# One tile ahead: out-projections before the norm, and the feed-forward part's first product before the last casts

## The chip, the cores and the metric

The program runs on one core of one Trainium2 chip. The metric is the device time of one execution in microseconds, the median of several runs. The profile and all rows come from one execution of the kernel before.

## The reference

One layer of a hybrid streaming encoder over 2048 prompt tokens and 64 sample tokens (hidden size 1024), all in float32. Token mixing is sliding-window attention beside a chunked spatial gate; what follows it matters here:

```python
def _merge(attn_o, cmlp_o, norm_attn_g, norm_cmlp_g, w_out):
    cat = jnp.concatenate([_rmsnorm(attn_o, norm_attn_g), _rmsnorm(cmlp_o, norm_cmlp_g)], -1)
    return cat @ w_out

def _post(x, mix, ln1_g, ln1_b, w_gate_up, w_down, ln2_g, ln2_b):
    h = _layernorm(ALPHA * x + mix, ln1_g, ln1_b)
    gu = h @ w_gate_up
    f = (jax.nn.silu(gu[..., :D_FF]) * gu[..., D_FF:]) @ w_down
    return _layernorm(ALPHA * h + f, ln2_g, ln2_b)
```

The feed-forward width D_FF is 2816.

## The kernel before, in words

Tokens come in 17 tiles: 16 of 128 prompt tokens and one of 64 sample tokens (tile 16). Every float32 product is done as three fp32r matmuls on operands that are split into a high and a low part: ScalarE (ACT) casts the high part, VectorE (DVE) or GpSimd (POOL) subtracts it for the low part (`split`, L108 and L109; the three matmuls are L154, L155 and L156 in `mm3`).

The program runs in three stages. The first does the projection, the attention and the gate, to about 510 us of the span. The second, of the functions called m2, does the out-projection and the first layer norm tile by tile, to about 707 us. The third is the feed-forward part over four blocks of tokens; it forms its first matmul by seven half-size products in the manner of Strassen (`product`), in an order held in a list, `order`.

The order is written by hand: the kernel runs in a mode in which each engine executes its instructions in the order in which the Python code issues them. An engine that waits for a semaphore holds everything behind it on that engine.

For each tile t the second stage does these steps:

- `m2_load(t)`: SyncE's queue (SP) brings the merged heads and x into `catx` (L601, L602).
- `m2_split(t)`: for each of eight pieces k, ACT writes the high part of the operand `cathl` (L614), DVE the low part (L615).
- `m2_mm(t, n)`: half n of the out-projection, 24 matmuls into two PSUM banks `po` (six banks serve this tag).
- `m2_add(t, n)`: ACT scales x (L629), DVE adds the two banks (L630, L631).
- `m2_ln(t)`: the norm on DVE (L638 to L645), with a power on POOL (L88). `m2_gains` makes its gain and bias rows, `gb`, by transposes (PE L658) and copies (ACT L659).
- `m2_T(t)`: PE transposes the normed tile, `catx`, into `hTp` (L671, eight transposes), ACT copies it out (L672, twice) and issues two DMAs on its own queue (L675 writes h_d, L676 hy_d). The text calls this step T and its tile: T0, T12.

Before the loop stand mm(2,1), the gains, the adds of tile 2 and split(3). In the loop (L1106 before), iteration t does mm(t) with its adds (from t = 3 on), ln(t), load(t+2), T(t-1) and split(t+2):

```python
    for t in range(NT - 4):
        if t > 2:
            for n in range(2):
                m2_mm(t, n)
                m2_add(t, n)
        m2_ln(t)
        nx = {0: None, 1: 4, 2: None}.get(t, t + 2)
        if nx:
            m2_load(nx)
        if t:
            m2_T(t - 1)
        if nx:
            m2_split(nx)
```

From t = 6 on each iteration also does four of `prep_steps`: loads, subtractions on POOL and splits (`put`) that make the feed-forward part's operands, hf1 to hf7, out of h. The tail finishes tiles 13 to 16 among the first products. The last two of those steps are the put of hf3: two casts on ACT (L108) and two subtractions on DVE (L109). hf3 lies in the buffer of `gb`, so its casts wait for the last norm, L645 of tile 16. Products 1, 6 and 7 share one PSUM bank, accA; after products 1 and 6 ACT copies it out (L859 into a0 and a1) before the next may write it. In that tail `order[0]` is product 1, `order[1]` 5, `order[2]` 6, `order[3]` 2 and `order[4]` 7 of the first output tile, and `order[5]` is product 1 of the second.

Of the kernel before, what the change touches and what calls it, by code (L numbers as in the profile page):

```python
# [20 lines left out]
NT = 17  # L21
# [17 lines left out]
def rows(t):  # L39
    return P if t < NP else DEC  # L40
# [3 lines left out]
def hybrid_step(ctx: ExitStack, tc: tile.TileContext, x_prompt, x_sample, xT_prompt, xT_sample, cache_kT, cache_v, w_in,  # L44
# [105 lines left out]
    def mm3(out, parts):  # L150

        n = len(parts)
        for i, ((ah, al), (bh, bl)) in enumerate(parts):
            nc.tensor.matmul(out, ah, bh, start=(i == 0), stop=False)  # L154
            nc.tensor.matmul(out, ah, bl, start=False, stop=False)  # L155
            nc.tensor.matmul(out, al, bh, start=False, stop=(i == n - 1))  # L156
# [437 lines left out]
    def of_f1(name, dt, prod):  # L594

        return f1.tile([P, 8 * NHX], dt, name=name, tag=f"hf{prod}", bufs=1)[:, :2 * D]
# [8 lines left out]
    def m2_split(t, ks=range(KD)):  # L605
        m = rows(t)
        s = cat_t[t][:, 0].rearrange("p (k q) -> p k q", q=P)
        if ks[0] == 0:
            xr_t[t] = (of_f1("cathl", F32R, 2).rearrange("p (s k q) -> p s k q", s=2, q=P) if t == 3 else
                       wp.tile([P, 2, KD, P], F32R, name="cathl", tag="W"))  # L610
        c = xr_t[t]
        for k in ks:
            gcol = vecT[:, 8 + k:9 + k]
            nc.scalar.activation(c[:, 0, k, :m], s[:, k, :m], AF.Copy, scale=gcol)  # L614
            nc.vector.scalar_tensor_tensor(out=c[:, 1, k, :m], in0=s[:, k, :m], scalar=gcol,  # L615
                                           in1=c[:, 0, k, :m].bitcast(F32), op0=ALU.mult, op1=ALU.subtract)

    def m2_mm(t, n):
        m = rows(t)
        c = xr_t[t]  # L620
        po = po_t[t, n] = [ps1.tile([P, 512], F32, name=f"po{h}", tag="x", bufs=6) for h in range(2)]
        for h in range(2):
            mm3(po[h][:m], [((c[:, 0, k, :m], c[:, 1, k, :m]), wo[n, k]) for k in range(4 * h, 4 * h + 4)])

    def m2_add(t, n):
        m = rows(t)
        ts_ = cat_t[t][:m, 1, n * 512:(n + 1) * 512]
        po = po_t.pop((t, n))
        nc.scalar.activation(ts_, ts_, AF.Copy, scale=ALPHA)  # L629
        nc.vector.scalar_tensor_tensor(out=ts_, in0=po[0][:m], scalar=rstd_a[:m, t:t + 1], in1=ts_, op0=ALU.mult, op1=ALU.add)  # L630
        nc.vector.tensor_tensor(out=ts_, in0=po[1][:m], in1=ts_, op=ALU.add)  # L631
# [17 lines left out]
    def m2_gains(v):  # L649

        if v == 0:
            gb = of_f1("gb", F32, 3)
            gb_t.update({0: gb[:, :D], 1: gb[:, D:]})
        for h in range(2):
            pt = ps1.tile([P, 4, P], F32, name="gbp", tag="pj")
            for j in range(4):
                c = 16 + 8 * v + 4 * h + j
                nc.tensor.transpose(pt[:, j], vecT[:, c:c + 1].to_broadcast([P, P]), ident)  # L658
            nc.scalar.activation(gb_t[v][:, h * 512:(h + 1) * 512], pt.rearrange("p j q -> p (j q)"), AF.Copy, scale=ALPHA)  # L659

    def m2_T(t):
        m = rows(t)
        tt = cat_t[t][:, 1]
        hT = cat_t[t][:, 0].rearrange("p (k q) -> p k q", q=P)
        if t == NT - 1:
            hT = f1.tile([P, KD, DEC], F32, name="hT", tag="hraw", bufs=4)
        for h in range(2):
            pt = ps1.tile([P, 4, P], F32, name="hTp", tag="pj")
            for j in range(4):
                k = 4 * h + j  # L670
                nc.tensor.transpose(pt[:, j, :m], tt[:m, k * P:(k + 1) * P], ident[:m, :m])  # L671
            nc.scalar.activation(hT[:, 4 * h:4 * h + 4, :m], pt[:, :, :m], AF.Copy, scale=1.0 / ALPHA)  # L672
        b = min(t // 4, NB - 1)
        o = (t - 4 * b) * P
        nc.scalar.dma_start(out=h_d[b][:, :, o:o + m], in_=hT[:, :, :m])  # L675
        nc.scalar.dma_start(out=hy_d[t][:m], in_=tt[:m])  # L676
        del cat_t[t]
# [111 lines left out]
    def slab_piece(key):  # L789
        tag = later.pop(0)  # L790
        return f1.tile([P, 4, P], F32, name="wsum", tag=tag, bufs=4 if tag == "hraw" else 2)
# [12 lines left out]
    def sums(b, i, keys=(5, 6, 7)):  # L804
        src = gu_src[b, i]
        for key, x, y, op in ((5, "u0", 4, ALU.add), (6, 5, 1, ALU.subtract), (7, 1, "u0", ALU.subtract)):
            if key in keys:
                src[key] = slab_piece(key) if early else f2.tile([P, 4, P], F32, name="wsum", tag="wsum", bufs=3)
                nc.gpsimd.tensor_tensor(out=src[key], in0=src[x], in1=src[y], op=op)
# [27 lines left out]
    def tmp(name):  # L837
        if early:
            return slab("tmp", 2, lambda: f1.tile([P, 2, NHX], F32, name=name, tag="hraw", bufs=4))
        return f2.tile([P, NHX], F32, name=name, tag="tmp", bufs=6)  # L840

    def product(b, i, prod):
        n = TB[b] // 2
        w, h = wf.pop((b, i, prod)), forms[b, prod]
        bank = {1: "A", 6: "A", 7: "A", 4: "A", 2: "B", 5: "C", 3: "C"}[prod]
        new = prod in (1, 2, 5)
        if new:
            acc[i, bank] = ps1.tile([P, 512], F32, name=f"acc{bank}", tag="x", bufs=6)
        ps = acc[i, bank][:, :n]
        for k in range(4):  # L850
            wh, wl, hh, hl = w[:, 0, k], w[:, 1, k], h[:, 0, k, :n], h[:, 1, k, :n]

            nc.tensor.matmul(ps, wh, hh, start=(new and k == 0), stop=False, skip_group_check=not new)  # L853
            nc.tensor.matmul(ps, wh, hl, start=False, stop=False, skip_group_check=not new)  # L854
            nc.tensor.matmul(ps, wl, hh, start=False, stop=(k == 3), skip_group_check=not new)  # L855

        def keep(key):
            part[i, key] = tmp(key)
            nc.scalar.copy(part[i, key][:, :n], ps)  # L859

        def add(key, to):
            part[i, key] = a = part.pop((i, to))
            nc.vector.tensor_tensor(out=a[:, :n], in0=ps, in1=a[:, :n], op=ALU.add)

        def out(sh, g, u):
            nc.vector.tensor_tensor(out=g, in0=u, in1=g, op=ALU.mult)  # L866
            f = ff[b, i][:, :, sh * n:(sh + 1) * n]
            split(f[:, 0], f[:, 1], g)

        if prod == 1:  # L870
            keep("a0")
        elif prod == 6:
            keep("a1")
        elif prod == 7:
            keep("a2")
            part[i, "c22"] = a = part.pop((i, "a2"))
            nc.vector.tensor_tensor(out=a[:, :n], in0=acc[i, "C"][:, :n], in1=a[:, :n], op=ALU.add)
        elif prod == 2:
            add("c11", "a0")
            g = part[i, "c11"][:, :n]  # L880
            nc.scalar.activation(g, g, AF.Silu)
        elif prod == 4:
            ff[b, i] = f2.tile([P, 4 * NHX], F32R, name="ff", tag="ff", bufs=4)[:, :4 * n].rearrange("p (s t) -> p s t", s=2)
            out(0, part.pop((i, "c11"))[:, :n], ps)
        elif prod == 3:
            add("c12", "a1")
            g = part.pop((i, "c12"))[:, :n]
            nc.scalar.activation(g, g, AF.Silu)
            out(1, g, part.pop((i, "c22"))[:, :n])
# [210 lines left out]
    m2_gains(0)  # L1100
    m2_mm(2, 1)
    m2_gains(1)
    m2_add(2, 0)
    m2_add(2, 1)
    m2_split(3)
    for t in range(NT - 4):  # L1106
        if t > 2:
            for n in range(2):
                m2_mm(t, n)
                m2_add(t, n)  # L1110
        m2_ln(t)
        nx = {0: None, 1: 4, 2: None}.get(t, t + 2)
        if nx:
# [5 lines that stand above are left out]
        if t == 4:  # L1119

            nc.scalar.activation(warm, neg_half, AF.Silu)
        if t == 6:
            prep = [f for _, f in sorted(prep_steps(0), key=lambda e: e[0])]
        if t >= 6:
            for _ in range(4):
                prep.pop(0)()
        if t in (NT - 10, NT - 7):
            load_gu(0, (t - NT + 10) // 3)
# [30 lines left out]
    m2_mm(16, 1)  # L1159
    m2_add(16, 1)  # L1160
    m2_ln(16)
    prep.pop(0)()
    prep.pop(0)()
    sums(0, 1, (5, 6))
    store_forms(0)
    product(*order[0])
    m2_T(15)
    product(*order[1])
    product(*order[2])
    m2_T(16)  # L1170
    product(*order[3])
    product(*order[4])
# [299 lines left out]
```

## Time and profile before

| what | us |
|---|---|
| median of three runs | 2186.68 |
| the runs | 2186.68, 2185.61, 2188.88 |
| the profiled execution | 2188.62 |
| its span | 2186.8 |
| busy in the span: PE / DVE / ACT / POOL | 2106.3 / 1482.2 / 943.3 / 571.4 |

The profiled execution's own time is 1.9 us above the median and 1.8 us above its span. Times in rows are counted from the start of the span. A row of a timeline gives the start and the length of a group of instructions, and in brackets how long the engine was idle before it and what released it. A matmul's row shows its whole length; matmuls are pipelined, so the next one starts before it ends. PEclk is TensorE's granted clock as a share of full speed: 1.00 is 2.4 GHz, 0.50 is 1.2 GHz.

### The profile page before, as it was taken

How to read it: one execution, taken by the hardware profiler on the slowest of the kernel's cores; microseconds unless marked ns; L12 is line 12 of the kernel's file. 1: busy time of each engine (PE TensorE's matmuls, PEld its weight loads, DVE VectorE, ACT ScalarE, POOL GpSimd, SP SyncE). 2: the span in 40 equal slices, each digit the busy share in tenths (PEclk: the TensorE clock that was granted, in tenths of full speed). 3: DMA queues.
4: the chain of work that ended last, by engine and by line, in shares of the span. 5: the costliest groups of instructions: out<-in, count | busy, mean ns of one | idle time of the engine just before them, and what ended most of it. 6: DMA issues, size and time to landing. Idle time of an engine off the chain costs nothing.

```text
span 2186.8 us, 35667 instructions
## 1 busy us (share of the span) xinstructions
PE 2106.3 (96%) x13219; PEld 1890.2 (86%) x13219; DVE 1482.2 (68%) x2899; ACT 943.3 (43%) x2255; POOL 571.4 (26%) x508
## 2 busy tenths in 40 slices
PE   8999999987998899999999999999999999999998
PEld 6888888866887799999989999989999998999996
DVE  6877777786798677887765555675555576444446
ACT  6666666663443444444433333433333342333333
POOL 0222222231123556665212221121221121111110
PEclk9999999988999999999999999999999999999999
DMA  5111111043554767777777677785776776555652
GB/s 198 39 39 40 39 40 39 27 160 121 193 199 157 289 238 237 287 259 255 271 259 249 237 255 233 262 290 198 271 247 231 240 259 244 188 193 188 191 194 92
DMA packets 172942, 418.27 MB, mean 191 GB/s; under 512 B 20800, under 2 KB 51264, under 8 KB 172768
## 3 DMA queue, kind: packets, MB, share of 16 engines
q1 hardware_dynamic: 152240, 397.31, 52.7%
q10 hardware_dynamic: 20352, 18.35, 2.5%
q8 instruction: 104, 1.70, 0.3%
q14 instruction: 70, 0.57, 0.1%
q0 software_dynamic: 176, 0.33, 0.1%
HBM read 328.31 MB, written 87.62 MB: 190 GB/s over the span
## 4 chain that ended last, share of the span: by engine, by line
PE 78%; DVE 13%; ACT 4%; issue 2%; DMA 1%; POOL 1%; SPq 0%; ACTq 0%; DVEq 0%; POOLq 0%
PE accA L853 8%; PE accA L855 7%; PE accA L854 7%; PE pd L154 7%; PE pd L155 7%; PE pd L156 7%; PE accC L853 4%; PE accC L854 4%; PE accC L855 4%; PE po L154 3%; PE po L155 3%; PE po L156 3%; PE pj L154 2%; PE pj L156 2%; PE pj L155 2%
## 5 line engine op out<-in xcount | busy, mean ns | idle before, releaser
L109 POOL TENSOR_TENSOR wf<-guraw,wf 128x512 fp32r<-128x512 f32 x173 | 249.3, 1441 | 812.2 <-ACT wf L108 740.4
L853 PE MATMUL accA<-hf,wf 128*128 128x256 f32 (+1 forms) x1408 | 407.7, 290 | 26.0 <-ACT a L859 23.2
L855 PE MATMUL accA<-hf,wf 128*128 128x256 f32 (+1 forms) x1408 | 404.6, 287 | 0.5 <-DVE wf L109 0.5
L854 PE MATMUL accA<-hf,wf 128*128 128x256 f32 (+1 forms) x1408 | 402.5, 286 | 0.0
L1210 DVE TENSOR_TENSOR y<-pd,y 128x512 f32<-128x512 f32 (+1 forms) x354 | 243.1, 687 | 166.0 <-PE pd L156 164.3
L853 PEld LDWEIGHTS accA<-hf,wf 128*128 128x128 f32 x1408 | 266.6, 189 | 38.0 <-ACT a L859 27.0
L154 PE MATMUL pd<-wd,ff 128*128 128x512 f32 (+1 forms) x708 | 280.4, 396 | 0.0
L155 PE MATMUL pd<-wd,ff 128*128 128x512 f32 (+1 forms) x708 | 280.1, 396 | 0.0
L156 PE MATMUL pd<-wd,ff 128*128 128x512 f32 (+1 forms) x708 | 278.9, 394 | 0.0
L854 PEld LDWEIGHTS accA<-hf,wf 128*128 128x128 f32 x1408 | 267.7, 190 | 8.2
L855 PEld LDWEIGHTS accA<-hf,wf 128*128 128x128 f32 x1408 | 266.5, 189 | 0.9 <-DVE wf L109 0.9
L109 DVE TENSOR_TENSOR wd<-draw,wd 128x512 fp32r<-128x512 f32 x176 | 171.5, 975 | 53.7 <-ACT wd L108 48.2
L854 PE MATMUL accC<-hf,wf 128*128 128x256 f32 (+1 forms) x704 | 201.5, 286 | 2.6 <-DVE hf L109 2.6
L853 PE MATMUL accC<-hf,wf 128*128 128x256 f32 (+1 forms) x704 | 202.9, 288 | 0.0
L859 ACT COPY a<-accA 128x256 f32<-128x256 f32 (+1 forms) x264 | 99.6, 377 | 238.9 <-PE accA L855 233.3
L855 PE MATMUL accC<-hf,wf 128*128 128x256 f32 (+1 forms) x704 | 202.2, 287 | 0.0
L108 ACT CAST ff<-a 128x256 fp32r<-128x256 f32 (+1 forms) x176 | 72.7, 413 | 290.2 <-DVE a L866 285.7
L108 ACT CAST wf<-guraw 128x512 fp32r<-128x512 f32 x264 | 163.2, 618 | 7.9 <-PE po L156 2.9
L156 PEld LDWEIGHTS pd<-wd,ff 128*128 128x128 f32 (+1 forms) x708 | 131.4, 186 | 33.7
L154 PEld LDWEIGHTS pd<-wd,ff 128*128 128x128 f32 (+1 forms) x708 | 131.6, 186 | 18.0
L155 PEld LDWEIGHTS pd<-wd,ff 128*128 128x128 f32 (+1 forms) x708 | 131.8, 186 | 16.3
L109 DVE TENSOR_TENSOR ff<-a,ff 128x256 fp32r<-128x256 f32 (+1 forms) x176 | 88.5, 503 | 84.6 <-ACT ff L108 84.6
(275 smaller groups left out, 4816.1 us busy)
## 6 DMA issues: line engine op xcount, KB each, us to landing
wf<-wf_d SPq DMA_DIRECT2D x264, 512.0 KB, 4.6
guraw<-in_w_gate_up_dram SPq DMA_DIRECT2D x110, 512.0 KB, 6.1
wf_d<-wf SPq DMA_DIRECT2D x88, 512.0 KB, 5.0
draw<-in_w_down_dram SPq DMA_DIRECT2D x176, 256.0 KB, 4.7
guraw<-in_w_gate_up_dram SPq DMA_DIRECT2D x66, 256.0 KB, 6.7
hraw<-h_d SPq DMA_DIRECT2D x36, 256.0 KB, 5.7
x<-in_xT_prompt_dram SPq DMA_DIRECT2D x32, 256.0 KB, 3.2
catx<-cat_d SPq DMA_DIRECT2D x16, 512.0 KB, 3.8
```

Of the source, the lines that this page charges most:

```text
L108: nc.scalar.copy(hi, src)
L109: (on or nc.vector).tensor_tensor(out=lo, in0=src, in1=hi.bitcast(F32), op=ALU.subtract)
L154: nc.tensor.matmul(out, ah, bh, start=(i == 0), stop=False)
L155: nc.tensor.matmul(out, ah, bl, start=False, stop=False)
L156: nc.tensor.matmul(out, al, bh, start=False, stop=(i == n - 1))
L853: nc.tensor.matmul(ps, wh, hh, start=(new and k == 0), stop=False, skip_group_check=not new)
L854: nc.tensor.matmul(ps, wh, hl, start=False, stop=False, skip_group_check=not new)
L855: nc.tensor.matmul(ps, wl, hh, start=False, stop=(k == 3), skip_group_check=not new)
L859: nc.scalar.copy(part[i, key][:, :n], ps)
L1210: nc.vector.tensor_tensor(out=y, in0=pd[:m], in1=y, op=ALU.add)
```

## The change

In the loop's lead-in split(3) comes ahead of the adds of tile 2. In the loop the out-projections run one tile ahead: mm(3) stands in iteration 0, the halves of mm(4) in iterations 2 and 3, and from t = 4 on iteration t does the adds of tile t and then both halves of mm(t+1), ahead of ln(t). In the tail the first product goes ahead of the put of hf3, which now stands behind the third; the sums of two weight pieces on POOL are issued behind T15 in place of ahead of product 1. Lines behind L1105 are counted three higher after the change.

```diff
--- before.py
+++ after.py
@@ -1100,14 +1100,17 @@
     m2_gains(0)
     m2_mm(2, 1)
     m2_gains(1)
+    m2_split(3)
     m2_add(2, 0)
     m2_add(2, 1)
-    m2_split(3)
+
+    ahead = {0: [(3, 0), (3, 1)], 2: [(4, 0)], 3: [(4, 1)], NT - 5: []}
     for t in range(NT - 4):
         if t > 2:
-            for n in range(2):
-                m2_mm(t, n)
-                m2_add(t, n)
+            m2_add(t, 0)
+            m2_add(t, 1)
+        for e in ahead.get(t, [(t + 1, 0), (t + 1, 1)] if t > 2 else []):
+            m2_mm(*e)
         m2_ln(t)
         nx = {0: None, 1: 4, 2: None}.get(t, t + 2)
         if nx:
@@ -1159,14 +1162,14 @@
     m2_mm(16, 1)
     m2_add(16, 1)
     m2_ln(16)
-    prep.pop(0)()
-    prep.pop(0)()
-    sums(0, 1, (5, 6))
     store_forms(0)
     product(*order[0])
     m2_T(15)
+    sums(0, 1, (5, 6))
     product(*order[1])
     product(*order[2])
+    prep.pop(0)()
+    prep.pop(0)()
     m2_T(16)
     product(*order[3])
     product(*order[4])
```

**TensorE around T2.** First before: the last matmuls of mm(3,1) (operand cathl_6263), T2 (hTp_6433 and hTp_6439 from catx_5929) and the first matmul of mm(4,0) (operand cathl_6319).

```order
L154 MATMUL po1_6391<-wo11h_5969,cathl_6263 128x512
L155 MATMUL po1_6391<-wo11l_5970,cathl_6263 128x512
L156 MATMUL po1_6391<-wo11h_5969,cathl_6263 128x512
L671 MATMUL hTp_6433<-ident_212,catx_5929 128x128 [waits DVE_49,Activation_49]
L671 MATMUL hTp_6433<-ident_212,catx_5929 128x128 x3
L671 MATMUL hTp_6439<-ident_212,catx_5929 128x128 [waits Activation_49]
L671 MATMUL hTp_6439<-ident_212,catx_5929 128x128 x3
L154 MATMUL po0_6464<-wo00h_5610,cathl_6319 128x512
```

Now with the change: the last matmuls of mm(4,1) (operand cathl_6371), T2 (hTp_6485 and hTp_6491), and the first of mm(5,0), whose operand is cathl_6499.

```order
L154 MATMUL po1_6446<-wo11h_5969,cathl_6371 128x512
L155 MATMUL po1_6446<-wo11l_5970,cathl_6371 128x512
L156 MATMUL po1_6446<-wo11h_5969,cathl_6371 128x512
L671 MATMUL hTp_6485<-ident_212,catx_5929 128x128 [waits Activation_49]
L671 MATMUL hTp_6485<-ident_212,catx_5929 128x128 x3
L671 MATMUL hTp_6491<-ident_212,catx_5929 128x128 [waits Activation_49]
L671 MATMUL hTp_6491<-ident_212,catx_5929 128x128 x3
L154 MATMUL po0_6522<-wo00h_5610,cathl_6499 128x512 [waits DVE_49,Activation_49]
L155 MATMUL po0_6522<-wo00l_5611,cathl_6499 128x512
L156 MATMUL po0_6522<-wo00h_5610,cathl_6499 128x512 [waits DVE_49]
```

Behind T2 stands the product of tile 5 and no longer that of tile 4, and its first matmuls wait for ACT and DVE.

**ScalarE around T2, with the change.** The copies of T2 (from hTp_6485 and hTp_6491), its two DMA issues, the split of tile 5 (cathl_6499) and the scaling of tile 4's x for its add (catx_6354).

```order
L672 ACTIVATE catx_5929<-hTp_6485 128x512 [waits PE_49]
L672 ACTIVATE catx_5929<-hTp_6491 128x512 [waits PE_49]
L675 DMA h_d0_87<-catx_5929 1024x1x128 [waits Activation_49]
L676 DMA hy_d2_93<-catx_5929 128x1024 [waits DMAHW1_49,DVE_49]
L614 ACTIVATE cathl_6499<-catx_6482,vecT_224 128x128 [waits DMAHW4_49,DMAHW3_49,DMAHW2_49]
L614 ACTIVATE cathl_6499<-catx_6482,vecT_224 128x128 x7
L629 ACTIVATE catx_6354<-catx_6354 128x512 x2
```

These rows stand in the same order as before; what moved is the product on TensorE that uses cathl_6499.

**ScalarE in the tail.** First before: the scaling of tile 16's x (catx_7617), the casts of hf3, the copy behind product 1 (a0 from accA), T15 (hTp_7861, hTp_7867), the copy behind product 6, and the first copy of T16 (hT).

```order
L629 ACTIVATE catx_7617<-catx_7617 64x512
L108 CAST hf3_7834<-hraw_7004 128x512 [waits DVE_49]
L108 CAST hf3_7834<-hraw_7008 128x512
L859 COPY a0_7859<-accA_7846 128x256 [waits PE_49]
L672 ACTIVATE catx_7539<-hTp_7861 128x512 [waits PE_49]
L672 ACTIVATE catx_7539<-hTp_7867 128x512 [waits PE_49]
L675 DMA h_d3_90<-catx_7539 1024x1x128 [waits Activation_49]
L676 DMA hy_d15_106<-catx_7539 128x1024
L859 COPY a0_7859<-accA_7846 128x256 [waits PE_49]
L672 ACTIVATE hT_7901<-hTp_7902 128x256 [waits DVE_49,PE_49]
```

Now with the change, from the same scaling on.

```order
L629 ACTIVATE catx_7617<-catx_7617 64x512
L859 COPY a0_7850<-accA_7837 128x256 [waits PE_49]
L672 ACTIVATE catx_7539<-hTp_7852 128x512 [waits PE_49]
L672 ACTIVATE catx_7539<-hTp_7858 128x512 [waits PE_49]
L675 DMA h_d3_90<-catx_7539 1024x1x128 [waits Activation_49]
L676 DMA hy_d15_106<-catx_7539 128x1024 [waits DVE_49]
L859 COPY a0_7850<-accA_7837 128x256 [waits PE_49]
L108 CAST hf3_7896<-hraw_7056 128x512 [waits DVE_49]
L108 CAST hf3_7896<-hraw_7060 128x512
L672 ACTIVATE hT_7901<-hTp_7902 128x256 [waits DVE_49,PE_49]
```

The casts moved from ahead of the copy behind product 1 to behind the copy behind product 6, and so to right ahead of T16's copies.

## Rows read from the trace of the kernel before

All rows are of the profiled execution; times are us from the span's start.

**Rows 1.** The page: busy time by engine, and the chain's shares.

```profile
PE 2106.3 (96%) x13219; PEld 1890.2 (86%) x13219; DVE 1482.2 (68%) x2899; ACT 943.3 (43%) x2255; POOL 571.4 (26%) x508
...
PE 78%; DVE 13%; ACT 4%; issue 2%; DMA 1%; POOL 1%; SPq 0%; ACTq 0%; DVEq 0%; POOLq 0%
```

**Rows 2.** TensorE's waits: us in total, times, longest.

```profile
PE accA L853 <- ACT a L859: 23.2, 14, 5.1
PE hTp L671 <- DVE catx L645: 13.6, 2, 11.0
```

**Rows 3.** PE timeline, 516 to 541 (start, length; idle before it in brackets).

```profile
516.95 1.03 PE L658 MATMUL gbp<-ident,vecT 128*128 128x128 f32 x8
528.95 1.94 PE L671 MATMUL hTp<-ident,catx 128*128 128x128 f32 x8 [10.96 <-DVE catx L645]
533.49 1.94 PE L671 MATMUL hTp<-ident,catx 128*128 128x128 f32 x8 [2.61 <-DVE catx L645]
535.09 0.78 PE L154 MATMUL po<-wo00h,cathl 128*128 128x512 f32 x1
```

**Rows 4.** ScalarE's timeline, 516 to 540, same columns.

```profile
517.59 1.08 ACT L659 ACTIVATE gb<-gbp 128x512 f32<-128x512 f32 x2 [4.86 <-PE gbp L658]
...
519.59 2.43 ACT L614 ACTIVATE cathl<-catx,vecT 128x128 fp32r<-128x128 f32 x8
```

**Rows 5.** VectorE's timeline, 517 to 536.

```profile
524.16 1.28 DVE L638 BATCH_NORM_STATS2 hst<-catx 128x6 f32<-128x512 f32 x2
...
527.51 1.28 DVE L645 SCALAR_TENSOR_TENSOR catx<-catx,hrs,gb 128x1024 f32<-128x1024 f32 x1 [0.45 <-POOL hrs L88]
```

**Rows 6.** ScalarE's timeline behind T2, 545 to 566 (ACTq: its DMA issues).

```profile
548.44 1.09 ACT L672 ACTIVATE catx<-hTp 128x512 f32<-128x512 f32 x2 [9.66 <-PE hTp L671]
...
550.17 0.62 ACTq L676 DMA_DIRECT2D hy_d<-catx  x1
550.91 2.45 ACT L614 ACTIVATE cathl<-catx,vecT 128x128 fp32r<-128x128 f32 x8 [1.39 <-DVE rs_e L87]
```

**Rows 7.** The chain, 545 to 566 (start, us, what): T2 and T3.

```profile
547.96 0.87 PE hTp L671 x8
...
559.74 0.87 PE hTp L671 x8
```

**Rows 8.** PE timeline, 653 to 664: T11 and T12.

```profile
653.76 1.03 PE L671 MATMUL hTp<-ident,catx 128*128 128x128 f32 x8
...
662.29 1.06 PE L671 MATMUL hTp<-ident,catx 128*128 128x128 f32 x8 [2.04 <-ACT catx L629]
```

**Rows 9.** ScalarE's timeline, 645 to 664: split(13).

```profile
648.69 2.45 ACT L614 ACTIVATE cathl<-catx,vecT 128x128 fp32r<-128x128 f32 x8 [4.98 <-DMA catx<-cat_d]
```

**Rows 10.** ScalarE's timeline in the tail, 704 to 727.

```profile
710.75 1.14 ACT L108 CAST hf<-hraw 128x512 fp32r<-128x512 f32 x2 [9.67 <-DVE catx L645]
```

**Rows 11.** PE timeline in the tail, 704 to 726: product 6, T16, order[5].

```profile
712.21 0.58 PE L853 MATMUL accA<-hf,wf 128*128 128x256 f32 x1 [5.08 <-ACT a L859]
...
715.07 1.11 PE L671 MATMUL hTp<-ident,catx 64*128 64x64 f32 x8
...
720.26 0.39 PE L853 MATMUL accA<-hf,wf 128*128 128x256 f32 x1 [0.98 <-ACT wf L108]
```

**Rows 12.** PE timeline in the feed-forward part: two waits of nearly one length.

```profile
1102.75 0.58 PE L853 MATMUL accA<-hf,wf 128*128 128x256 f32 x1 [2.85 <-ACT a L859]
...
1455.21 0.39 PE L853 MATMUL accA<-hf,wf 128*128 128x256 f32 x1 [2.84 <-ACT a L859]
```

**Rows 13.** Windows (us, busy by engine, PEclk, DMA share, GB/s).

```profile
517.00:529.00 12.00, 1.04 (x10) 0.83 (x9) 9.13 (x19) 4.44 (x12) 1.52 (x1) 0.69 0.38 151
...
640.00:703.00 63.00, 60.96 (x290) 48.05 (x289) 57.14 (x97) 25.78 (x62) 16.31 (x11) 1.00 0.52 176
...
1102.00:1105.00 3.00, 2.25 (x10) 2.25 (x11) 2.93 (x7) 1.49 (x4) 2.36 (x2) 0.50 0.94 358
...
1455.00:1458.00 3.00, 2.79 (x18) 2.57 (x19) 3.00 (x4) 0.95 (x3) 2.90 (x2) 1.00 0.98 369
```

## The prediction

> **What bounds the kernel now.** I read the page first, then TensorE's waits, then the timelines of the two stretches that the change touches. TensorE (PE) is busy 96% of the span and carries 78% of the chain that ended last [rows 1]: time is gained only where PE waits, and lost wherever a new PE wait appears. The waits [rows 2] name the two spots at which the change aims: hTp behind DVE's catx (13.6 us, 11.0 the longest) is the hole ahead of the first norms, and the 5.1 us maximum of accA behind ScalarE's L859 is in the tail.
>
> The hole [rows 3]: PE ends gbp near 518, waits 10.96 us for the first norm, does T0, waits 2.61 us, does T1, and only then begins the out-projection mm(3,0), at 535.09. Meanwhile the operand of mm(3,0) had long been made: ScalarE begins its eight L614 at 519.59 [rows 4]. The granted clock fell in the hole (mean 0.69 from 517 to 529 [rows 13]), and PE is slow behind it: T1 with the 48 matmuls of mm(3) takes from 533.49 to 547.96, 14.47 us, where the later blocks take 11.78 [rows 3, 7]. The difference, 2.69 us, is what one fall of the clock cost here (0.73 in T1, about 2.0 in the matmuls).
>
> In the steady loop there is no PE wait: a block is 0.87 us of transposes and 10.91 us of matmuls (48 at 0.227), and one follows another every 11.78 us [rows 7]. Look at ScalarE behind the transposes [rows 6]: T's copies start 0.48 us after T, then two DMA issues, and the first L614 of the next split starts only at 550.91, 2.95 us after T's start. Today nobody feels this, since that operand is used a whole block later.
>
> **The change, part by part.**
>
> *The out-projections move one tile ahead.* The first L614 of split(3) now starts right behind the gains' copies, at 517.59 + 1.08 = 518.67 [rows 4]; with 0.34 us for it (a group of eight takes 2.45, plus the hand-over) mm(3,0) starts at 519.0. ScalarE makes a piece every 0.31 us, PE uses one in 0.68, so both halves run at full rate: 10.9 us, to 529.9. DVE still does eight L615 and four adds ahead of the first norm, in the other order, so T0's data are ready at about 528.8 as before [rows 5], under cover of the matmuls. T0 runs 529.9 to 530.8.
>
> Now the new wait. In the new order mm(t+2,0) stands on PE directly behind T(t-1), but its operand's L614 stand on ScalarE behind T(t-1)'s two copies and two DMA issues. From T's start to the first finished L614 is 2.95 + 0.34 = 3.3 us; T itself takes 0.87, so PE waits 2.45 us [rows 6, 7]. What is queued behind it on PE is the whole next block. So mm(4,0) runs 533.2 to 538.7, T1 to 539.5. mm(4,1) needs a PSUM bank of the six that mm(3) and mm(4,0) fill; the first comes free with add(3,0), whose L629 stands behind T1's copies and issues: 538.7 + 2.95 + 0.6 (L629) + 0.75 (L630) = 543.0, a wait of 3.5 us. Then mm(4,1) to 548.5, T2 to 549.4, a wait of 2.45, mm(5) 551.9 to 562.8, T3 to 563.7. Before, T3 and mm(5) were both done at 547.96 + 2 x 11.78 = 571.52. At this point the changed kernel is **7.8 us ahead**.
>
> Each block from mm(6) to mm(12) then lasts 0.87 + 2.45 + 10.91 = 14.2 instead of 11.78 us. Seven of them cost 17.2: mm(12) ends at 562.8 + 7 x 14.23 = 662.4 (it was 653.8, at T11's start [rows 8]). In these blocks PSUM is no limit: L614, one L629 and one L630 take 3.8 us, inside the 5.4 of mm(t+2,0). SP's order is unchanged, and load(t+2) writes into a slot that mm(t,1) freed a whole block earlier.
>
> The loop's end costs once more. T12 waits for the norm of tile 12, and its adds stand on ScalarE behind split(13), which now comes after T10, the first thing after mm(12). Before, split(13) started at 648.69 and T12 at 662.29, 13.6 us later [rows 8, 9]. Now it starts at 662.4 + 2.95 = 665.4, so T12 starts at 679.0: **+16.7 us**, all of the above included. PE has only T10, T11 and mm(13,1) to do meanwhile and is idle some 7 us, where it waited 2.04. The hole of 10.96 us made it slow; I charge the same fall here: **+2.7**. From T12 on no order changes until the tail.
>
> *The tail.* Before, ScalarE stood at hf3's casts until 710.75 [rows 10], because hf3 lies in the buffer of the gains that the last norm reads, and product 1's copy L859 was queued behind them; product 6 began at 712.21 and slowly, T16 at 715.07, order[5] at 720.26 [rows 11]. Now the copy goes first, product 6 runs under the last norm, and T16 starts when that norm ends, 710.75. ScalarE's casts then stand ahead of T16's copies, but those still end well before product 7, so order[5] keeps its distance of 5.2 us from T16: 715.07 - 710.75 = **-4.3 us**. The sums on POOL are only written later; their order there is the same. What follows moves rigidly: the feed-forward's waits come to 23.2 us in 14 [rows 2], and those hang on PE's own products, so they can't absorb a shift.
>
> *The clock at the new waits.* A fall at a boundary costs the 2.0 us of its matmuls from above. Whether it falls the trace answers both ways: after a wait of 2.85 us at 1102.75 the granted clock was 0.50 (1.2 GHz), after 2.84 us at 1455.21 it was 1.00 (2.4 GHz) [rows 12, 13]; after 2.04 us and T12's transposes, 3.1 us without a product, it stayed 1.00 [rows 8, 13]. A boundary, with 3.3 us without a product, lies among these, and I take a fall at 3 of the 9 equal ones (**+6.0**; bounds 0 and 18) and one at the 3.5 us wait of mm(4,1) (**+2.0**).
>
> The Trainium skill, in "TensorE: Matmul & The Clock Gate", Part 4: PE-mode transpose, says that transposes don't count as PE work for the clock in the way matmuls do. It speaks against this change: by it every boundary would look idle through transposes and wait, all nine would fall, and the sum would be 12 us higher than mine; T12's row speaks against so strict a reading.
>
> **Sum**: 16.7 + 2.7 - 4.3 + 6.0 + 2.0 = +23.1 us. On the profiled execution, 2188.6 us, that is 2211.7; this execution lies 1.9 above the median of the runs, 2186.68, from which I forecast **2210 us**.
>
> **Rivals.**
> - *No boundary falls.* 16.7 + 2.7 - 4.3 = +15.1: 2202. For it: 1455.21 and T12. Against: 1102.75.
> - *Nearly all fall.* 15.1 + 2.0 + 18 = +35: 2222. For it: each boundary is the same, so one answer may hold for all; against: T12. The skill's rule above gives this case.
> - *The other side: the boundary wait is covered.* If L614 did not have to stand behind T's copies and issues, mm(5) would start at 529.9 + 13.5 = 543.4 instead of 560.6, all matmuls would move 17 us up, T12 (one transpose and the norm chain later) about 15, and with the tail's 4.3 the kernel would be 19.3 us faster: 2167. Between this and the no-fall case lie 34.4 us for a wait of 2.45, or 14 us for each us of it (nine boundaries, and the two late waits of the same making); the change loses from a wait of 1.4 us on. Against: ScalarE's program order puts the split there, and the 2.95 us stand in every block.
> - *The DMA issues don't hold ScalarE.* Then L614 starts at 548.44 + 1.09 = 549.53 rather than 550.91, the wait is 1.07, and the change comes to -19.3 + 15.0 = -4.3: 2182. Against: L614 starts 0.12 us after the second issue ends [rows 6]. For: there it was in no hurry.
>
> **How the numbers follow.** Forecast case (one to six boundaries fall) 0.55, none 0.17, nearly all 0.14, covered 0.06, issues that don't hold 0.08. The range 2200 to 2222 takes in the first three except the end of the third, and leaves out the last two. A measurement can tell about 0.2%, 4.4 us, from no change: the covered case and a part of the fourth are faster, 0.09; the rest of the fourth is the same, 0.05; slower 0.86.
>
> **What would show it.** Right: mm(3,0) near 519 and no 11 us hTp wait; po behind ACT's cathl L614 among PE's waits, nine times about 2.4 us; T's spacing 14 us; T12 near 679 or later with a wait of some 7 us; in the tail T16 right after the last L645. A granted clock of 0.50 behind some boundaries, blocks of over 15 us there, show falls; their number sets the end. Wrong: T's spacing still 11.8 us, L614 starting ahead of L675, or a tail as long as before.

## The result and the profile after

The changed kernel takes 2216.98 us (median of four runs, 2213.08 to 2218.73) against 2187.51: a ratio of 1.0133, 95% interval 1.0115 to 1.015, or 29.5 us more. The forecast was 2210 us in a range of 2200 to 2222. The execution profiled has a span of 2216.7 us, 29.9 above that of before.

TensorE's waits with the change (us in total, times, longest) answer to [rows 2]:

```profile
PE po L154 <- ACT cathl L614: 23.8, 10, 2.6
PE accA L853 <- ACT a L859: 15.9, 15, 2.8
...
PE hTp L671 <- ACT catx L629: 6.7, 1, 6.7
...
PE po L154 <- DVE catx L630: 3.5, 1, 3.5
```

The 11 us hole is gone. In its place stand ten waits of an out-projection for its operand's casts, 23.8 us together, one of 3.5 us for a PSUM bank, and 6.7 us at T12 (and 0.7 us behind T8 for a low part, L615). The PE timeline in the early stretch (start, length; idle before it in brackets) answers to [rows 3]:

```profile
517.97 0.47 PE L154 MATMUL po<-wo00h,cathl 128*128 128x512 f32 x1 [1.07 <-issue]
...
528.98 1.03 PE L671 MATMUL hTp<-ident,catx 128*128 128x128 f32 x8
532.54 0.50 PE L154 MATMUL po<-wo00h,cathl 128*128 128x512 f32 x1 [2.52 <-ACT cathl L614]
...
539.72 1.03 PE L671 MATMUL hTp<-ident,catx 128*128 128x128 f32 x8
544.22 0.75 PE L154 MATMUL po<-wo01h,cathl 128*128 128x512 f32 x1 [3.46 <-DVE catx L630]
```

mm(3,0) starts at 517.97 (535.09 before), under the norm, as meant; the hole is filled. Then each of T0 to T9 is followed by a wait. Three blocks later, T4 to T6:

```profile
583.50 1.03 PE L671 MATMUL hTp<-ident,catx 128*128 128x128 f32 x8
587.05 0.50 PE L154 MATMUL po<-wo00h,cathl 128*128 128x512 f32 x1 [2.52 <-ACT cathl L614]
...
598.10 1.03 PE L671 MATMUL hTp<-ident,catx 128*128 128x128 f32 x8
601.70 0.50 PE L154 MATMUL po<-wo00h,cathl 128*128 128x512 f32 x1 [2.57 <-ACT cathl L614]
...
614.32 1.03 PE L671 MATMUL hTp<-ident,catx 128*128 128x128 f32 x8
```

From T4 to T5 are 14.60 us and from T5 to T6 16.22, against 11.78 in [rows 7]. The wait is the same (2.52 and 2.57), so the second block lost 1.62 us in something else. The windows of the two blocks (us, busy by engine from PE on, PEclk, DMA share, GB/s) show what:

```profile
583.00:598.00 15.00, 12.48 (x59) 10.18 (x59) 9.23 (x18) 4.58 (x12) 1.45 (x1) 1.00 0.63 210
598.00:614.00 16.00, 13.43 (x57) 10.82 (x56) 10.24 (x18) 4.57 (x12) 4.94 (x3) 0.89 0.60 198
```

The granted clock was 1.00 in the first and 0.89 on average in the second, which holds a piece at half rate (1.2 GHz). ScalarE behind T4 answers to [rows 6], in the same order and with the same gaps:

```profile
584.14 1.09 ACT L672 ACTIVATE catx<-hTp 128x512 f32<-128x512 f32 x2 [8.70 <-PE hTp L671]
...
585.93 0.62 ACTq L676 DMA_DIRECT2D hy_d<-catx  x1
586.60 2.45 ACT L614 ACTIVATE cathl<-catx,vecT 128x128 fp32r<-128x128 f32 x8 [1.38 <-issue]
```

T4 starts at 583.50, the next operand's first cast at 586.60, 3.1 us later, as before: there T2 starts at 547.80 in PE's timeline and the cast at 550.91 [rows 6].

```profile
547.80 1.04 PE L671 MATMUL hTp<-ident,catx 128*128 128x128 f32 x8
```

But before, nobody waited for that cast. T10, T12 and the tail answer to [rows 8, 11]:

```profile
678.54 1.03 PE L671 MATMUL hTp<-ident,catx 128*128 128x128 f32 x8
```

```profile
694.46 1.94 PE L671 MATMUL hTp<-ident,catx 128*128 128x128 f32 x8 [6.68 <-ACT catx L629]
```

```profile
738.50 1.04 PE L671 MATMUL hTp<-ident,catx 128*128 128x128 f32 x8
...
744.71 0.68 PE L671 MATMUL hTp<-ident,catx 64*128 64x64 f32 x8 [2.29 <-DVE catx L645]
...
750.92 0.39 PE L853 MATMUL accA<-hf,wf 128*128 128x256 f32 x1 [0.98 <-ACT wf L108]
```

T12 starts 32.2 us later than before (662.29) and T15, at 738.50, 33.8 later; T16 comes 29.6 later and order[5] 30.7 (720.26 before). So the loop loses 32.2, the slow clock behind T12 another 1.7, and the tail gives 3.2 back.

### The profile page after: what moved, and what is told of

Same layout as the page of the kernel before. It is cut to its first block, busy times and chain, and to the rows that moved or that the text cites. A ratio compares the mean times of both kernels' runs of the same rounds, so it can differ in the third digit from the quotient of the medians.

```text
span 2216.7 us, 35666 instructions
## 1 busy us (share of the span) xinstructions
PE 2121.2 (96%) x13219; PEld 1898.0 (86%) x13219; DVE 1484.5 (67%) x2899; ACT 943.7 (43%) x2255; POOL 570.2 (26%) x508
## 4 chain that ended last, share of the span: by engine, by line
PE 75%; DVE 14%; ACT 5%; issue 3%; DMA 2%; POOL 1%; ACTq 0%; SPq 0%; DVEq 0%; POOLq 0%
PE accA L853 7%; PE accA L855 7%; PE accA L854 7%; PE pd L154 7%; PE pd L155 7%; PE pd L156 7%; PE accC L854 3%; PE accC L853 3%; PE accC L855 3%; PE po L154 3%; PE po L156 3%; PE po L155 3%; PE pj L156 2%; PE pj L155 2%; PE pj L154 2%
## 5 line engine op out<-in xcount | busy, mean ns | idle before, releaser
L109 POOL TENSOR_TENSOR wf<-guraw,wf 128x512 fp32r<-128x512 f32 x173 | 249.5, 1442 | 811.7 <-ACT wf L108 741.6
L853 PE MATMUL accA<-hf,wf 128*128 128x256 f32 (+1 forms) x1408 | 407.5, 289 | 18.8 <-ACT a L859 15.9
L109 DVE TENSOR_TENSOR wd<-draw,wd 128x512 fp32r<-128x512 f32 x176 | 173.5, 986 | 53.3 <-ACT wd L108 47.8
L156 PEld LDWEIGHTS pd<-wd,ff 128*128 128x128 f32 (+1 forms) x708 | 131.6, 186 | 33.8
L109 DVE TENSOR_TENSOR ff<-a,ff 128x256 fp32r<-128x256 f32 (+1 forms) x176 | 88.4, 502 | 84.6 <-ACT ff L108 84.6
```

What stands on the lines that cost most here:

```text
L109: (on or nc.vector).tensor_tensor(out=lo, in0=src, in1=hi.bitcast(F32), op=ALU.subtract)
```

## The experiments

**The two parts apart.** `tail_alone` is the kernel before with the tail's part of the diff alone, `loop_alone` the changed kernel with the old tail.

> Only the tail's part of the change, on the kernel before: product 1 and its copy go ahead of hf3's casts, the loop is as before. My sum gave this part -4.3 us; in the changed kernel's trace T16 came 4.2 us earlier relative to T15, but the two products behind it ran at the slow clock, and order[5] kept only 3.2. If the parts simply add: about 2183 to 2184.5 us against 2187.5, T16 right at the end of the last L645, the 5.1 us wait of accA gone. If the tail's gain is swallowed later (a rival: the feed-forward part is paced by its loads), 2187.5.

> Only the loop's part of the change, the tail as before. If all of the loss is the loop's, and the parts add: 2217 + 3 to 4 = 2220 to 2221 us, with ten waits of po behind ACT's cathl of 2.5 us, T12 some 32 us later than in the kernel before, and the 5.1 us wait of accA back. If the tail's new order is to blame for a part of the loss: under 2217.

tail_alone: 2182.25 us against 2187.52, ratio 0.9979 (0.997 to 0.9988). loop_alone: 2219.78, ratio 1.015 (1.0136 to 1.0164). The tail's part gains 5.3 us (2.6 to 6.6 by its interval) and the loop's costs 32.3, together 27.0, within the interval of the change itself (25 to 33 us). Both medians lie a little below what I expected, by 0.8 and 0.2 us. PE's tail, T15 before and then T15, T16 and order[5] in tail_alone:

```profile
704.66 1.04 PE L671 MATMUL hTp<-ident,catx 128*128 128x128 f32 x8
```

```profile
703.69 1.04 PE L671 MATMUL hTp<-ident,catx 128*128 128x128 f32 x8
...
709.89 0.68 PE L671 MATMUL hTp<-ident,catx 64*128 64x64 f32 x8 [2.29 <-DVE catx L645]
...
716.11 0.38 PE L853 MATMUL accA<-hf,wf 128*128 128x256 f32 x1 [0.98 <-ACT wf L108]
```

T16 runs as soon as the last norm ends, and order[5] starts 12.4 us behind T15; before it was 15.6 (704.66 to 720.26). So in the trace, too, order[5] gains 3.2 us over T15; T15 itself is 1.0 us earlier, as is already T2 (546.83 against 547.80), where nothing was changed. The gain of the tail is real, and the loss is the loop's alone: in loop_alone T12 starts at 692.62, and the 5.08 us wait of accA is back.

**The split ahead of T.** `split_first` moves one call in the changed kernel's loop:

```diff
-        if t:
-            m2_T(t - 1)
         if nx:
             m2_split(nx)
+        if t:
+            m2_T(t - 1)
```

> The changed kernel with one move: in each iteration the split of tile t+2 is issued ahead of T(t-1) and not behind it, so that ScalarE makes the next operand ahead of T's copies and DMA issues. My theory (the boundary wait is ScalarE's order and nothing else): the ten waits of po behind cathl go, T's spacing is 11.8 us, the clock stays at 1.00 from T2 on, T12 waits little; the wait of mm(4,1) for add(3) stays (3.5 us, with a fall of about 2). Some 2168 to 2176 us, so faster than both kernels. Rival 1 (the loads of tile t+2 come too late once they are wanted earlier): PE waits show the DMA of catx behind the split, 2185 or more. Rival 2 (transposes count as idle for the clock, whatever the wait): spacing stays above 12 us with slow matmuls behind each T, 2185 to 2195.

It takes 2193.45 us, ratio 1.0023 (1.0014 to 1.0032): 23.5 us better than the change, and still not better than the kernel before. PE's timeline:

```profile
551.42 1.03 PE L671 MATMUL hTp<-ident,catx 128*128 128x128 f32 x8
...
563.19 1.03 PE L671 MATMUL hTp<-ident,catx 128*128 128x128 f32 x8
...
574.97 1.03 PE L671 MATMUL hTp<-ident,catx 128*128 128x128 f32 x8
```

From T2 to T5 the spacing is 11.77 to 11.79 us, so the waits behind cathl were indeed ScalarE's order, and a transpose does not slow a block by itself: rival 2 falls. Not every wait went: mm(4,0) waited 2.35 us for the low part (L615), mm(4,1) the expected 3.46. And my number fell. From T5 on ScalarE itself stands (its waits, us, times, longest):

```profile
ACT cathl L614 <- DMA hy_d<-catx: 31.1, 7, 7.7
```

`catx` and `cathl` take their buffers from one pool of 14, eight of which the out-projection's weights hold. The split now wants one earlier than T's store has left it, seven times. ScalarE waited 7.3 us more for the load of tile 13, with T10's copies queued behind that split, and T11 waited 3.1 us for those; T12 started only at 670.53, 8.2 us later than before. VectorE was not what held T12 here: from 640 to 660 it was busy 14.5 of 20 us.

**The clock by itself.** `filled_wait` leaves the changed kernel's order and gives PE work in the pause, ten matmuls whose result the product behind them overwrites:

```diff
+        for j in range(fill):
+            nc.tensor.matmul(po[0], xr_t[t - 1][:, 0, j % KD], wo[n, 0][0], start=True, stop=True)
...
-            m2_mm(*e)
+            m2_mm(*e, fill=10 if t > 1 and e[1] == 0 else 0)
```

> The changed kernel with ten more matmuls (128x512, results overwritten) at each boundary from mm(4,0) to mm(12,0), of the operand of the tile before, into the bank that the product behind them starts afresh: 2.3 us of work in a wait of 2.5 us. The boundary stays, the idleness goes. If the falls of the clock at 7 of 9 boundaries are what lies between my sum and the result (about 1.7 us each): no fall at any boundary, T's spacing 14.3 to 14.7 us everywhere, about 2205 us (2202 to 2209). If the slow matmuls behind the boundaries have another cause, or the falls cost nothing: 2217 or more, since the work added is on PE's queue. mm(4,1)'s wait is not filled and may still be followed by a fall.

2206.35 us, ratio 1.0089 (1.0075 to 1.0103): 10.6 us less than the changed kernel, by added work.

```profile
607.21 1.03 PE L673 MATMUL hTp<-ident,catx 128*128 128x128 f32 x8
...
610.78 0.50 PE L154 MATMUL po<-wo00h,cathl 128*128 128x512 f32 x1 [0.25 <-ACT cathl L614]
...
621.83 1.03 PE L673 MATMUL hTp<-ident,catx 128*128 128x128 f32 x8
```

```profile
600.00:650.00 50.00, 48.45 (x222) 39.09 (x221) 37.52 (x67) 15.83 (x40) 15.27 (x10) 1.00 0.52 176
```

T's spacing from T2 on is 14.50 to 14.62 us (once 15.66, with 0.78 us behind L615) and the clock 1.00 (the window below the rows; from 550 to 600 too), with the operand as late as before (607.21 to 610.78 is 3.57 us; 3.55 above). The blocks of 16.2 us in the changed kernel are blocks of 14.6 with a fall. This shows the second part of the loss: not the pause, but what the clock does behind it.

**What the pause is made of.** `dma_off_act` issues T's two stores for tiles 0 to 9 on SyncE's queue:

```diff
-        nc.scalar.dma_start(out=h_d[b][:, :, o:o + m], in_=hT[:, :, :m])
-        nc.scalar.dma_start(out=hy_d[t][:m], in_=tt[:m])
+        q = nc.sync if t < 10 else nc.scalar
+        q.dma_start(out=h_d[b][:, :, o:o + m], in_=hT[:, :, :m])
+        q.dma_start(out=hy_d[t][:m], in_=tt[:m])
```

> The changed kernel with the two stores of T issued on SyncE's queue for tiles 0 to 9, no longer on ScalarE's; order and work are otherwise the same. My theory (the boundary wait is made of T's copies and the two issues, one behind the other on ScalarE): the wait of po behind cathl falls from 2.5 to 1.1 or 1.2 us (the issues' 1.4 us go), T's spacing is about 13.2 us; with so short a pause I expect no fall at the boundaries either. 9 x 1.4 + 7 x 1.6 + 1.4 each at mm(4,1) and T12 = 26.6 us less at most: 2190 to 2194. Rival (the issues cost ScalarE nothing, the wait is the copies and the split alone): 2217, waits 2.5 as before. Rival 2 (SyncE's queue now stands behind T, and the loads of the next tiles with it): new waits on the DMA of catx, 2200 or more.

2198.21 us, ratio 1.005 (1.0034 to 1.0065): 18.8 us less than the change, and 4 us more than I expected.

```profile
562.66 1.03 PE L671 MATMUL hTp<-ident,catx 128*128 128x128 f32 x8
564.72 0.50 PE L154 MATMUL po<-wo00h,cathl 128*128 128x512 f32 x1 [1.03 <-ACT cathl L614]
...
575.75 1.03 PE L671 MATMUL hTp<-ident,catx 128*128 128x128 f32 x8
```

The wait is 1.03 us and the spacing 13.09: two DMA issues held ScalarE 1.5 us in each block. So the rival by which the issues don't hold ScalarE is wrong by this run as well. No boundary shows a fall (the clock is 1.00 from 560 to 656); behind mm(4,1)'s wait, now 2.04 us, it still fell. T12 came 22.9 us earlier than with the change; 3 us of that were lost behind the tail, in a part that I did not follow up.

**A version meant to keep the gain.** `ahead_then_back` fills the hole and then returns to the old order. The loop's core:

```diff
+    m2_mm(3, 0)
+    m2_mm(3, 1)
+    m2_ln(0)
+    m2_load(4)
+    m2_split(4)
+    m2_T(0)
+    m2_mm(4, 0)
+    m2_ln(1)
+    m2_add(3, 0)
+    m2_T(1)
+    m2_mm(4, 1)
+    m2_ln(2)
+    m2_add(3, 1)
+    m2_load(5)
+    m2_split(5)
+    m2_T(2)
+    for t in range(4, NT - 4):
+        if t < 7:
+            m2_mm(t + 1, 0)
+            m2_add(t, 0)
+            m2_mm(t + 1, 1)
+            m2_add(t, 1)
+            m2_ln(t - 1)
+            if t == 6:
+                m2_ln(t)
+            m2_load(t + 2)
+            m2_split(t + 2)
+            m2_T(t - 1)
+            if t == 6:
+                m2_T(t)
...
```

> A version meant to beat both: the tail as in the change; in the loop the out-projections run one tile ahead from tile 3 to tile 7 only, with split(t+2) ahead of T(t-1) on ScalarE and ahead of the next norm on VectorE, and add(3) ahead of T1; behind mm(7) T5 and T6 stand together and the order of the kernel before goes on from there with split behind T a whole block ahead of its use. If the loss is ScalarE's and VectorE's order at the boundaries, no PE wait over 1 us is left between the gains and T12, the clock stays at 1.00, and T6 ends near 578 to 580 (595.9 in the kernel before): 16 to 17 us from the loop and 5.3 from the tail, about 2165 us (2163 to 2172). Rival (the early blocks are bound by VectorE's norms or by late loads of catx once the hole is filled): PE waits behind L645 or L615 of 2 to 5 us, 2172 to 2180, still faster than the kernel before.

2183.5 us, ratio 0.9984 (0.9975 to 0.9992), and so no better than the tail's part alone. First T6 in the chain of the kernel before (start, us, what), then T5 and T6, T11 and T12, and the split of tile 13 on ScalarE in ahead_then_back:

```profile
595.05 0.87 PE hTp L671 x8
```

```profile
578.15 1.04 PE L671 MATMUL hTp<-ident,catx 128*128 128x128 f32 x8
582.29 1.94 PE L671 MATMUL hTp<-ident,catx 128*128 128x128 f32 x8 [3.11 <-DVE catx L645]
```

```profile
646.04 1.06 PE L671 MATMUL hTp<-ident,catx 128*128 128x128 f32 x8 [0.41 <-DVE catx L645]
...
659.14 1.94 PE L671 MATMUL hTp<-ident,catx 128*128 128x128 f32 x8 [6.56 <-ACT catx L629]
```

```profile
646.25 2.45 ACT L614 ACTIVATE cathl<-catx,vecT 128x128 fp32r<-128x128 f32 x8 [10.84 <-DMA catx<-cat_d]
```

```profile
580.00:600.00 20.00, 16.50 (x73) 13.75 (x74) 14.71 (x29) 8.86 (x20) 5.75 (x4) 0.91 0.74 255
600.00:620.00 20.00, 20.00 (x94) 16.57 (x93) 18.56 (x33) 9.13 (x24) 4.75 (x4) 1.00 0.71 236
620.00:640.00 20.00, 19.42 (x92) 15.44 (x91) 18.72 (x34) 7.23 (x17) 5.69 (x4) 1.00 0.33 104
```

Here the reading turns. mm(7) is done at 578.15, T5's start; before it was done at T6's start, 595.05 in the chain (594.89 in the timeline). Less T5, which is still to do here, some 16 us of the hole's time were won. At T6 PE waits 3.1 us for VectorE's norm, T11 is 7.7 us ahead of before (653.76), and T12 only 3.1 (662.29). The windows say why: VectorE is busy 18.6 and 18.7 of 20 us from 600 to 640. It is the second bound of this loop, hardly behind PE, and PE's lead runs into it; in the kernel before it was as busy there (19.1 and 18.4 of 20 us) while PE never waited. T12 itself needs VectorE's norm: its row names L629, but that is tile 13's, on which T12 doesn't depend, and the norm's last instruction, L645, runs from 656.72 to 659.00, just ahead of T12.

Not all of VectorE's time is its own work. It waited 4.1 us, to 588.38, for ScalarE's L629 behind T6's copies and issues, and 0.8 us for the split of tile 13, whose load came late (the 10.84 us above): that load stands on SyncE's queue behind one of `prep_steps`, which waited 19.8 us there for a subtraction on VectorE (L109).

The 3.1 us of lead went too: behind the 6.56 us wait the clock was slow, and T15 came at 703.93, in tail_alone at 703.69.

`puts_on_pool` and `puts_earlier` test that, both on ahead_then_back:

```diff
-            split(o[:, 0], o[:, 1], t[key, kk])
+            split(o[:, 0], o[:, 1], t[key, kk], None if prod == 3 else nc.gpsimd)
```

```diff
-        if t == 6:
+        if t == 5:
             prep = [f for _, f in sorted(prep_steps(0), key=lambda e: e[0])]
-        if t >= 6:
+        if 5 <= t < 12:
```

> ahead_then_back with the low parts of hf1, hf5, hf6, hf7, hf2 and hf4 (the L109 of put, twelve of them ahead of T12, about 0.69 us each on VectorE) on GpSimd. In ahead_then_back VectorE is busy 18.6 of 20 us from 600 to 640, and T12 waits 6.6 us for a chain of split(13), adds and norm. If VectorE bounds that stretch and GpSimd's work beside it is free: T12 up to 8 us earlier (651 to 655) and some 2177 to 2180 us. If GpSimd's work beside VectorE slows VectorE as much as it takes off it (one L645 beside POOL's L699 took 2.3 us in place of 1.28): T12 at 658 or later, 2183 or more.

> ahead_then_back with the feed-forward part's operand steps (loads, subtractions, puts) one iteration earlier, so that some of VectorE's work moves from 600 to 660, where it is busy 93%, to 560 to 600, where it has 5 us free in 20. If VectorE bounds the stretch before T12: T12 1.5 to 3 us earlier (656 to 657.6), its wait shorter, 2180 to 2182 us. If the loads of h wait for T3's store and hold SyncE's queue ahead of load(7) or load(8): new waits on the DMA of catx, 2184 or more.

puts_on_pool: 2184.55 us, ratio 0.9988 (0.9979 to 0.9997). puts_earlier: 2180.27, ratio 0.9969 (0.9957 to 0.9981). One row each for T12, first puts_on_pool, then puts_earlier with a window of it:

```profile
661.62 1.94 PE L671 MATMUL hTp<-ident,catx 128*128 128x128 f32 x8 [5.92 <-ACT catx L629]
```

```profile
656.15 1.94 PE L671 MATMUL hTp<-ident,catx 128*128 128x128 f32 x8 [4.80 <-DVE catx L645]
```

```profile
580.00:600.00 20.00, 16.66 (x75) 13.96 (x76) 17.87 (x33) 9.10 (x21) 5.78 (x4) 0.91 0.84 287
```

Work taken off VectorE and given to GpSimd gained nothing: T12 came at 661.62, and VectorE was as busy as before (a window of it stands at the end). The same work moved to where VectorE had room (17.87 busy of 20 from 580 to 600, 14.71 before) brought T12 to 656.15, 3.0 us earlier. That fits VectorE's bound, but the steps that moved include loads and subtractions on POOL, and only 1.2 us of the 3.0 stood at T11 (644.82 against 646.04). Of the rest, 1.0 is L645 ahead of T12, which took 1.28 us with no subtraction on POOL beside it and 2.28 in ahead_then_back, and 0.8 the wait for the split of tile 13, which is gone. This version is the fastest measured, 6.9 us under the kernel before; tail_alone's interval overlaps it, so how much of that the loop gives beyond the tail's 5.3 us stays open.

## Why the prediction was right, and where it was off

- *The hole is filled.* Forecast: mm(3,0) at 519.0, T0 at 529.9 to run without a wait. Measured 517.97 and 528.98. Right.
- *A wait of 2.45 us at each boundary.* Measured 2.45 to 2.57, nine times, and 1.06 once more ahead of mm(13,1). These are counted from the end of T's row, 1.03 us long; on my count, from 0.87, they are about 2.7. The mechanism is shown by split_first and dma_off_act. From T to the first product I had 3.3 us and measured 3.55, and a block without a fall was 14.60 instead of 14.23: nine times 0.37 is 3.3 us that I left out. Of that 0.16 each time is a misreading: I took T2's start from the chain (547.96) and ScalarE's from its timeline, but PE's timeline has T2 at 547.80, so that L614 starts 3.11 us behind it and not 2.95.
- *mm(4,1) waits 3.5 us for add(3).* 3.46 us, with a fall, as forecast.
- *The number of falls.* This is the term that was mis-sized: I took 3 of 9, the trace shows 7 of 9 (blocks of 15.99 to 17.17 us behind T2, T3, T5, T6, T8 and T9, and T0 to T1 in 10.74 where filled_wait took 9.15; 0.7 of T8's 17.17 is the wait for L615; behind T4 and T7 14.60 and 14.61). The price of one was 1.6, not 2.0; the misreading just named makes 0.16 of that (mm(3) took 12.71 us in the timeline, 1.8 over 10.91). So 7 x 1.6 = 11.2 in place of 6.0. The range held, but seven is not in my main case of one to six falls (0.55); it is nearer to "nearly all", to which I gave 0.14. I leaned on T12's row, one case without a fall after 3.1 us without a product; the rule of the Trainium skill that I weighed against it ("TensorE: Matmul & The Clock Gate", Part 4: PE-mode transpose) came nearer: the trace agrees with it in seven boundaries and not in two. It doesn't show that transposes count as idle, since each boundary has its wait as well. And T12's row was no rule: in dma_off_act mm(4,1) starts after the same 3.1 us without a product, and there the clock fell.
- *T12.* Forecast 679.0 without falls, so 687 with mine; measured 694.46. The chain from T10 to T12 took 15.9 us (678.54 to 694.46) where I had 16.6, and PE's wait there was 6.68, forecast "some 7". Its fall cost 1.7, not 2.7.
- *The tail.* Forecast -4.3. T16 gained 4.2 over T15, as reasoned, but behind its wait of 2.29 us the clock fell: most matmuls of the next two products took 0.41 us in place of 0.28, and order[5] kept 3.2. That fall is what I left out. tail_alone shows the same 3.2 in its trace, and 5.3 in the medians.
- *The sum.* Mine, 23.1, against 29.9 between the two spans: 5.2 more for the falls and 3.3 for the boundaries, less 1.0 each at mm(3)'s start (the first stage ended 1.1 us earlier in this execution) and T12's fall, 0.7 in T12's chain, and the tail's 1.1 the other way. The rest, under 1 us, I don't assign.
- *The rivals.* "Covered" and "issues that don't hold ScalarE" both fell. "None falls" fell with the windows. The time I gave the second was too low as well: dma_off_act has its wait, 1.03 us, and took 2198 us where that rival says 2182. What no part of the prediction had is what stands right behind PE: VectorE's own work, on which ahead_then_back missed its number, and the buffers and the load of tile 13, on which split_first did. No version came near the 2167 of the covered case; whether one can is open.

## What to carry to other kernels

When a product is pulled ahead to fill a hole, look at what else its operand's maker does between the two new neighbours: here two copies and two DMA issues on the same engine came in between at each of nine boundaries, and a lead of some 16 us won once was paid with 2.8 us and more each time. Price a short recurring pause with the clock behind it, not by its length alone. And before filling a hole in the first engine, read the second engine's busy share in the stretch that follows: PE's lead of 16 us met VectorE and was down to 3 us at T12.

## What the runs showed of the hardware that I had not expected

- Pauses alike to 0.1 us did not decide the clock: behind the wait of 2.52 us at 587.05 it stayed at 1.00, behind that of 2.57 at 601.70 it fell. In six of the seven falls the first two to six matmuls behind the pause still ran at full rate (behind T2 none did), and some seven a little later started 0.43 us apart in place of 0.227, so that the row behind the wait alone does not show it. In the changed kernel's PE timeline behind T5:

```profile
602.04 0.39 PE L155 MATMUL po<-wo00l,cathl 128*128 128x512 f32 x1
...
602.64 0.63 PE L154 MATMUL po<-wo00h,cathl 128*128 128x512 f32 x1
603.07 0.63 PE L155 MATMUL po<-wo00l,cathl 128*128 128x512 f32 x1
...
606.38 0.39 PE L155 MATMUL po<-wo10l,cathl 128*128 128x512 f32 x1
```

- Added work made a program faster: ten useless matmuls in each of nine pauses took 10.6 us off the changed kernel.
- A subtraction on GpSimd beside VectorE gave VectorE no time back: its L645 took 2.30 us beside one and 1.28 without. The Trainium skill has this in "SBUF — State Buffer", Who interferes with whom: an instruction of VectorE with two inputs in SBUF contends with one of GpSimd that reads SBUF; the traces agree. So in puts_on_pool VectorE was busy 19.05 of 20 us from 620 to 640 with 26 instructions, in ahead_then_back 18.72 with 34. The window of puts_on_pool:

```profile
620.00:640.00 20.00, 18.82 (x88) 14.56 (x87) 19.05 (x26) 7.23 (x17) 12.56 (x9) 1.00 0.42 146
```
